# First mLSTM head: three gate projection groups issued ahead of chunk 0, each of the other nine queued on TensorE behind its own chunk

## The chip, the cores and the metric

The kernel runs on one core of one Trainium2 chip. The time is that of the device for one execution of the whole program, in microseconds; less is better. Before the change it is 1215.55 us, the median of 3 runs (1214.6 to 1216.65).

## The reference, cut to what matters

Two layers are computed on 1024 frames of a prompt and 32 frames of a running stream (1056 columns in all), width 1024. Layer 0 mixes pooling and band attention; the change doesn't touch it. Layer 1 is an mLSTM with four heads of width 256, in chunks (the kernel takes 128 frames at a time). For each head:

```
q, k, v, o, z, gates = split(rmsnorm(x) @ w_in)
b = cumsum(lf);  dmat = causal(b_t - b_s + ig_s);  m_t = max(b + m, max(dmat))
s = (q k^T) * exp(dmat - m_t)
num = a * (C q) + s v          # C: 256 x 256 state carried from chunk to chunk
h = num / max(|den|, exp(-m_t))
C = decay * C + (v * wgt)^T k
out = layernorm(h) * gain * sigmoid(o) * silu(z)
y = out @ w_out
```

The change is about the order of two kinds of TensorE work in the first head: the projections o and z (the gates of the output, needed only at the end of a head) and the chunks.

## The kernel before

Activations are kept feature-major, 128 features on the partitions and frames along the free dimension. A projection of 128 output features is done by `dense`: for each of three column groups (384, 384 and 288 frames) 24 matmuls accumulate in one PSUM bank of the pool pd (3 banks). These are 8 slices of the inner dimension, each in 3 products of high and low parts (`mm3`, L108 to L110). VectorE then takes the bank out. I call the 24 matmuls of one column group a group. Weights are loaded by `load_w`: two DMAs of 256 KB on SyncE's queue, two casts on ScalarE for the high part (L95), two subtractions for the low part on VectorE (L96); there are three buffers for them (wh, wl), so that the weights of a projection can be prepared when the projection three places ahead of it has run.

For one head of layer 1, program order is this:

- `head_qkv`: two projections each for q, k and v. After each k and each v projection `tokens` turns the result to frames on the partitions: for chunks 0 to 3, 4 to 7 and 8, it makes 4, 4 and 1 transposes on TensorE into the single bank of pool pm (L950), a copy by ScalarE (L953) and, for v, a subtraction by VectorE that forms the low part (L955). The bank is free for the next step only when the copy and the subtraction are done.
- `head_gate` puts the four gate projections o0, z0, o1, z1 on a list, as 12 steps of one group each (`later`). Nothing is issued yet. `fill` issues the next step of the list, and with a projection's first step the load of its weights.
- `head_mix`: nine chunks (the last with 32 frames). Each has the scores S (L1018: 4 matmuls), their product with the decay matrix D on VectorE, the split into a high part Sh (ScalarE, L1022) and a low part Sl (VectorE, L1023), the output pv from S and v and from the state Cp (9 matmuls, `mmv`, L985 to L987), and the state update pu (2 times 3 matmuls, `mmv`). D comes from an exponential on ScalarE (L1014) over a tile MA, which a DMA brings on SyncE's queue (3 buffers). At the end of each chunk `fill` issues one step of the list.
- `fill_all` issues what is left of the list (three steps), and `head_out` normalizes, transposes back and multiplies with the gates.

The order in which an engine issues instructions isn't program order. A planner goes through a model of the time line and lets each engine take, among the instructions that are ready in the model, the one that is earliest in program order. Steps that are later in the program but ready sooner run ahead. The order that results is fixed, and each engine keeps to it on the chip, waiting where an input is late. `tc.issue_after(ins)` takes that freedom away for one engine: what is traced inside it and runs on the engine of `ins` is placed behind `ins` in that engine's order; it doesn't wait for `ins` to end.

Other things that the prediction speaks of: q of the next head is written to the tile qT, of which there is one buffer, so q projections of head 1 can fill PSUM banks but not be taken out before head 0 has read its qT for the last time. z is written to a tile "row" (2 buffers), which v uses too ahead of its transposes.

Of the kernel before, what the change touches and what calls it, by code (L numbers as in the profile page):

```python
# [29 lines left out]
def clen(c):  # L30
    return 128 if c < 8 else DEC


class Net:
# [947 lines left out]
    def mmv(self, p, a, v, first, last):  # L982
        nc = self.nc
        (ah, al), (vh, vl) = a, v
        nc.tensor.matmul(out=p, lhsT=ah, rhs=vh, start=first, stop=False)  # L985
        nc.tensor.matmul(out=p, lhsT=ah, rhs=vl, start=False, stop=False)  # L986
        nc.tensor.matmul(out=p, lhsT=al, rhs=vh, start=False, stop=last)  # L987

    def head_mix(self, h, qT, kT, K, V):
        nc, io, lp = self.nc, self.io, self.lp  # L990
# [2 lines left out]
        st = lp.tile([128, NCH, 6], F32, name="bst", bufs=1)  # L993
        mv = lp.tile([128, NCH, 2], F32, name="bmv", bufs=1)
        C = Cp = None

        def split_C(C):
            Cp = self.split("C", [128, 2, VW], 2)
            nc.scalar.copy(out=Cp[0], in_=C)
            nc.vector.tensor_tensor(out=Cp[1], in0=C, in1=Cp[0].bitcast(F32), op=ALU.subtract)  # L1000
            return Cp
        for c in range(NCH):
            L = clen(c)
            t = slice(128 * c, 128 * c + L)
            if c == 8:
                C = lp.tile([128, 2, VW], F32, name="C", bufs=2)
                nc.sync.dma_start(out=C, in_=io["stC"][h].rearrange("(d p) v -> p d v", p=128))
                Cp = split_C(C)
            MA = lp.tile([128, 2, 128], F32, name="MA", bufs=3)
            nc.sync.dma_start(out=MA[:, :, :L], in_=self.mdr[h:h + 1, :, t].to_broadcast([128, 2, L]))  # L1010
            Mb, Ab = MA[:, 0, :L], MA[:, 1, :L]
            v = V[0][:L, c], V[1][:L, c]
            D = lp.tile([128, 128], F32, name="D", bufs=3)
            nc.scalar.activation(out=D[:L, :L], in_=Mb[:L], func=AF.Exp, scale=-1.0, bias=self.ct[:L, c, h:h + 1])  # L1014
            self.causal(D[:L, :L], L)
            ps = self.ps.tile([128, 512], F32, name="ps")
            for d in range(2):
                nc.tensor.matmul(out=ps[:L, :L], lhsT=kT[:, d, t], rhs=qT[:, d, t], start=(d == 0), stop=(d == 1))  # L1018
            S = lp.tile([128, 128], F32, name="S", bufs=2)
            Sp = [x[:L, :L] for x in self.split("S", [128, 128], 2)]  # L1020
            nc.vector.tensor_tensor(out=S[:L, :L], in0=ps[:L, :L], in1=D[:L, :L], op=ALU.mult)
            nc.scalar.copy(out=Sp[0], in_=S[:L, :L])  # L1022
            nc.vector.tensor_tensor(out=Sp[1], in0=S[:L, :L], in1=Sp[0].bitcast(F32), op=ALU.subtract)  # L1023
            pn = self.pv.tile([128, 512], F32, name="pv")[:L, 0:VW]
            self.mmv(pn, Sp, v, True, C is None)
            if C is not None:
                qa = lp.tile([128, 2, 128], F32, name="qa", bufs=2)
                qp = [x[:, :, :L] for x in self.split("qa", [128, 2, 128], 2)]
                for d in range(2):
                    nc.gpsimd.tensor_tensor(out=qa[:, d, :L], in0=qT[:, d, t], in1=Ab, op=ALU.mult)  # L1030
                nc.scalar.copy(out=qp[0], in_=qa[:, :, :L])  # L1031
                nc.gpsimd.tensor_tensor(out=qp[1], in0=qa[:, :, :L], in1=qp[0].bitcast(F32), op=ALU.subtract)  # L1032
                for d in range(2):
                    self.mmv(pn, (qp[0][:, d], qp[1][:, d]), (Cp[0][:, d], Cp[1][:, d]), False, d == 1)
            nc.scalar.copy(out=num[:L, c], in_=pn[:, 0:257])
            nc.vector.bn_stats(out=st[:, c], in_=num[:, c, 0:256])
            nc.vector.bn_aggr(out=mv[:, c], in_=st[:, c])
            wK = [x[:L] for x in self.split("wK", [128, 256], 2)]
            nc.scalar.mul(out=wK[0], in_=K[:L, c], mul=D[:L, L - 1:L])
            nc.vector.scalar_tensor_tensor(out=wK[1], in0=K[:L, c], scalar=D[:L, L - 1:L], in1=wK[0].bitcast(F32),  # L1040
                                           op0=ALU.mult, op1=ALU.subtract)
            Cn = lp.tile([128, 2, VW], F32, name="C", bufs=2)
            for d in range(2):
                ds = slice(128 * d, 128 * d + 128)
                pu = self.ps.tile([128, 512], F32, name="ps")[:, 0:VW]
                self.mmv(pu, (wK[0][:, ds], wK[1][:, ds]), v, True, True)
                if C is None:
                    nc.vector.tensor_copy(out=Cn[:, d], in_=pu)
                else:
                    nc.vector.scalar_tensor_tensor(out=Cn[:, d], in0=C[:, d], scalar=Ab[:, L - 1:L], in1=pu,  # L1050
                                                   op0=ALU.mult, op1=ALU.add)
            C = Cn
            if c < 7:
                Cp = split_C(C)
            self.fill()
            if c >= 7:
                nc.sync.dma_start(out=io["Co"][c - 7, h].rearrange("(d p) v -> p d v", p=128), in_=C[:, :, 0:257])
        return num, mv
# [232 lines left out]
```

## Time and profile before

| | |
|---|---|
| median of 3 runs | 1215.55 us (1214.6 to 1216.65) |
| the profiled execution's own time | 1215.28 us |
| its span in the profile | 1213.6 us |
| mean granted clock of TensorE | 0.991 of full speed |
| TensorE busy | 1183.3 us, 98% |
| VectorE, ScalarE, GpSimd busy | 681.2, 472.9, 298.9 us |

The span is that of the profiled execution; 1.7 us of its time lie around it. TensorE issues matmuls that overlap each other, so a matmul's duration is longer than its distance to the next, and a TensorE that is shown as busy isn't one at its peak. The granted clock is 1.00 at 2.4 GHz and 0.50 at 1.2 GHz.

### The profile page before, as it was taken

To read this page: it belongs to the slowest core of one execution; us is meant where nothing else is said; L and a number is where in the kernel's file an instruction comes from. 1 tells how busy PE (TensorE), PEld (TensorE's weight loads), DVE (VectorE), ACT (ScalarE), POOL (GpSimd) and SP (SyncE) were. 2 spreads that over 40 slices of the span, in tenths; PEclk is the share of its full clock that TensorE was granted. 3 is DMA by queue.
4 is the path that set the end of the run, shared out by engine and by line. 5 is a ranking of instruction groups with operands and counts; after the bars stand their busy time and mean duration, and the time that the engine had idled before them with its cause. 6 is when DMAs were issued, how large, how long until landed. Compare 5 with 4: busy or idle time off the path is not lost.

```text
span 1213.6 us, 19521 instructions
## 1 busy us (share of the span) xinstructions
PE 1183.3 (98%) x7457; PEld 1137.1 (94%) x7457; DVE 681.2 (56%) x1460; ACT 472.9 (39%) x980; POOL 298.9 (25%) x394
## 2 busy tenths in 40 slices
PE   7899999999999899999999999999999999999996
PEld 7899899898899799999999899999999999998996
DVE  7657476576668446774447533753247432666424
ACT  7624334443533454531334232432234322445521
POOL 1323532433241335620102300221003110123322
PEclk9999999999999999999999899999999999999998
DMA  8401121112212253321111231122111321122433
GB/s 257 125 19 54 54 82 53 54 45 67 78 36 92 80 176 105 124 94 53 54 36 53 63 101 36 52 67 98 36 51 42 76 88 36 44 77 79 128 104 130
DMA packets 79613, 94.03 MB, mean 77 GB/s; under 512 B 19208, under 2 KB 56856, under 8 KB 79520
## 3 DMA queue, kind: packets, MB, share of 16 engines
q1 hardware_dynamic: 79520, 92.79, 24.9%
q8 instruction: 58, 0.95, 0.3%
q14 instruction: 35, 0.29, 0.1%
HBM read 72.64 MB, written 21.69 MB: 78 GB/s over the span
## 4 chain that ended last, share of the span: by engine, by line
PE 95%; ACT 1%; DMA 1%; DVE 1%; issue 1%; POOL 1%; SPq 0%; DVEq 0%; POOLq 0%; ACTq 0%
PE pd L108 25%; PE pd L110 25%; PE pd L109 25%; PE pv L406 4%; PE ps L354 1%; PE pm L950 1%; PE ps L355 1%; PE ps L1018 1%; PE pv L985 1%; PE pv L987 1%; PE pv L986 1%; PE ps L985 1%; PE ps L986 1%; PE ps L987 1%; PE pm L176 1%
## 5 line engine op out<-in xcount | busy, mean ns | idle before, releaser
L108 PE MATMUL pd<-xh,wh 128*128 128x384 f32 (+1 forms) x1864 | 610.2, 328 | 9.4 <-ACT wh L95 7.8
L110 PE MATMUL pd<-xh,wl 128*128 128x384 f32 (+1 forms) x1864 | 607.5, 326 | 0.1
L109 PE MATMUL pd<-xl,wh 128*128 128x384 f32 (+1 forms) x1864 | 607.1, 326 | 0.1
L108 PEld LDWEIGHTS pd<-xh,wh 128*128 128x128 f32 x1864 | 352.4, 189 | 13.6 <-ACT wh L95 8.1
L109 PEld LDWEIGHTS pd<-xl,wh 128*128 128x128 f32 x1864 | 352.6, 189 | 2.6 <-POOL xl L203 0.3
L110 PEld LDWEIGHTS pd<-xh,wl 128*128 128x128 f32 x1864 | 352.3, 189 | 2.4 <-DVE wl L96 0.7
L95 ACT CAST wh<-wr 128x512 fp32r<-128x512 f32 x158 | 91.4, 619 | 154.6 <-PE pd L109 109.6
L96 DVE TENSOR_TENSOR wl<-wr,wh 128x512 fp32r<-128x512 f32 x116 | 78.2, 701 | 22.1 <-ACT wh L95 20.5
L96 POOL TENSOR_TENSOR wl<-wr,wh 128x512 fp32r<-128x512 f32 x42 | 55.7, 1342 | 83.4 <-DMA extr<-ext 27.4
L194 POOL TENSOR_TENSOR acc<-acc,sqt 128x384 f32<-128x384 f32 (+1 forms) x41 | 43.5, 1062 | 88.2 <-ACT sqt L193 88.1
L1032 POOL TENSOR_TENSOR qal<-qa,qah 128x256 fp32r<-128x256 f32 (+1 forms) x32 | 27.5, 863 | 141.1 <-ACT qah L1031 130.3
L75 POOL TENSOR_SCALAR_AFFINE_SELECT D<-D 128x128 f32<-128x128 f32 (+1 forms) x36 | 12.2, 340 | 181.2 <-ACT D L1014 168.1
L406 PE MATMUL pv<-st,vt 128*128 128x512 f32 (+1 forms) x192 | 55.1, 433 | 0.9 <-ACT rg L415 0.9
L406 PEld LDWEIGHTS pv<-st,vt 128*128 128x128 f32 x192 | 35.0, 189 | 20.3 <-issue 10.6
L263 DVE TENSOR_TENSOR row<-pd,r 128x384 f32<-128x384 f32 (+1 forms) x36 | 18.3, 520 | 59.4 <-PE pd L110 59.3
L372 ACT ACTIVATE st<-ps,far 128x256 f32<-128x256 f32 (+3 forms) x56 | 27.1, 489 | 50.0 <-DVE st L364 34.0
L1050 DVE SCALAR_TENSOR_TENSOR C<-C,MA,ps 128x258 f32<-128x258 f32 x64 | 30.4, 478 | 28.8 <-PE ps L987 17.8
L265 DVE SCALAR_TENSOR_TENSOR kT<-pd,r 128x384 f32<-128x384 f32 (+1 forms) x24 | 12.6, 524 | 57.4 <-PE pd L110 57.3
L395 DVE TENSOR_TENSOR st<-st,mb 128x512 f32<-128x512 f32 (+1 forms) x96 | 39.3, 485 | 8.3 <-POOL mb L699 8.3
L1030 POOL TENSOR_TENSOR qa<-qT,MA 128x128 f32<-128x128 f32 (+1 forms) x64 | 26.9, 439 | 66.1 <-DVE qT L263 35.9
L364 DVE TENSOR_TENSOR st<-ps,B 128x256 f32<-128x256 f32 (+1 forms) x72 | 25.3, 371 | 24.7 <-PE ps L355 24.3
L1085 ACT ACTIVATE hn<-num,n_u,n_y 128x256 f32<-128x256 f32 (+1 forms) x36 | 20.4, 596 | 40.9 <-PE pv L1087 34.3
(305 smaller groups left out, 1681.5 us busy)
## 6 DMA issues: line engine op xcount, KB each, us to landing
wr<-in_w SPq DMA_DIRECT2D x128, 256.0 KB, 3.0
xr<-mix SPq DMA_DIRECT2D x26, 192.0 KB, 2.5
wr<-in_w0o SPq DMA_DIRECT2D x16, 256.0 KB, 3.2
MA<-mdr SPq DMA_DIRECT2D x32, 128.0 KB, 3.5
wr<-in_w1o SPq DMA_DIRECT2D x16, 256.0 KB, 3.3
x<-in_x SPq DMA_DIRECT2D x16, 192.0 KB, 2.8
x<-x1d SPq DMA_DIRECT2D x16, 192.0 KB, 3.5
out_y<-y SPq DMA_DIRECT2D x16, 192.0 KB, 2.0
```

The lines of the kernel that those rows point to most:

```text
L95: nc.scalar.copy(out=wh[:, k], in_=wr)
L96: eng.tensor_tensor(out=wl[:, k], in0=wr, in1=wh[:, k].bitcast(F32), op=ALU.subtract)
L108: nc.tensor.matmul(out=p, lhsT=wh[:, k], rhs=xh[:, k], start=first and i == 0, stop=False)
L109: nc.tensor.matmul(out=p, lhsT=wh[:, k], rhs=xl[:, k], start=False, stop=False)
L110: nc.tensor.matmul(out=p, lhsT=wl[:, k], rhs=xh[:, k], start=False, stop=last and i == len(ks) - 1)
L194: (eng or nc.gpsimd).tensor_tensor(out=acc, in0=acc, in1=t[:, :n], op=ALU.add)
L372: nc.scalar.activation(out=st[:, off + a:off + b], in_=p[:, a:b], func=AF.Identity, bias=far)
L395: nc.vector.tensor_tensor(out=dst, in0=dst, in1=mb[:, a - q0:b - q0], op=ALU.subtract)
L406: nc.tensor.matmul(out=pv[:, a - q0:b - q0], lhsT=vt[:, j, 64 * e:64 * e + 128], rhs=dst, start=(i == 0), stop=(i == len(order) - 1))
L1030: nc.gpsimd.tensor_tensor(out=qa[:, d, :L], in0=qT[:, d, t], in1=Ab, op=ALU.mult)
L1032: nc.gpsimd.tensor_tensor(out=qp[1], in0=qa[:, :, :L], in1=qp[0].bitcast(F32), op=ALU.subtract)
L1050: nc.vector.scalar_tensor_tensor(out=Cn[:, d], in0=C[:, d], scalar=Ab[:, L - 1:L], in1=pu, op0=ALU.mult, op1=ALU.add)
```

## The change

Ahead of chunk 0 of the first head three steps of the list are issued in program order (the whole of o0). After that, each chunk of this head issues one step as before, but its matmuls are placed on TensorE behind the last matmul of the chunk's state update (`self.pe`, the last of the three of `mmv`). With nine chunks the twelve steps of the list are all gone at the end of chunk 8. Heads 1 to 3 stay as they were.

```diff
@@ mmv
-        nc.tensor.matmul(out=p, lhsT=al, rhs=vh, start=False, stop=last)
+        self.pe = nc.tensor.matmul(out=p, lhsT=al, rhs=vh, start=False, stop=last).ins
@@ head_mix
         C = Cp = None
+        if h == 0:
+            self.fill(3)
...
             if c < 7:
                 Cp = split_C(C)
-            self.fill()
+
+            with self.tc.issue_after(self.pe) if h == 0 else nullcontext():
+                self.fill()
             if c >= 7:
```

## Rows read from the trace of the kernel before

**Rows 1.** The page: span; chain that ended last, by engine.

```profile
span 1213.6 us, 19521 instructions
PE 95%; ACT 1%; DMA 1%; DVE 1%; issue 1%; POOL 1%; SPq 0%; DVEq 0%; POOLq 0%; ACTq 0%
```

**Rows 2.** Stretches of head 0: us, TensorE busy (matmuls), clock, DMA share, GB/s.

```profile
610.45:633.84 23.39, 22.74 (x145) 1.00 0.13 46
655.90:674.50 18.60, 18.60 (x139) 1.00 0.16 45
674.50:682.75 8.25, 5.23 (x31) 0.82 0.62 166
```

**Rows 3.** Waits of TensorE from 580 to 720 us: total, times, longest.

```profile
PE pv L985 <- ACT Sh L1022: 2.4, 2, 1.8
PE pd L108 <- DVE row L276: 0.7, 1, 0.7
PE ps L985 <- DVE S L1021: 0.6, 1, 0.6
```

**Rows 4.** Stretches of 2 us at the end of head 0's chunks, TensorE.

```profile
676.00:678.00 2.00, 0.29 (x3) 1.00 0.80 248
678.00:680.00 2.00, 1.89 (x14) 0.93 0.47 99
680.00:682.00 2.00, 1.49 (x6) 0.50 0.98 249
682.00:684.00 2.00, 1.88 (x6) 0.50 0.25 81
684.00:686.00 2.00, 2.00 (x8) 0.50 0.35 116
686.00:688.00 2.00, 2.00 (x11) 0.87 0.76 59
```

**Rows 5.** Time line of ScalarE around chunk 7: start, us, idle before and releaser.

```profile
677.47 0.40 ACT L1014 ACTIVATE D<-MA,g_c 128x128 f32<-128x128 f32 x1 [2.23 <-DMA MA<-mdr]
677.77 0.28 ACT L1022 CAST Sh<-S 128x128 fp32r<-128x128 f32 x1
```

**Rows 6.** Time line of VectorE: q of head 1 taken out of PSUM.

```profile
679.08 1.34 DVE L263 TENSOR_TENSOR qT<-pd,r 128x384 f32<-128x384 f32 x3
```

**Rows 7.** Time line of TensorE: o0's last matmul, transposes, chunk 0's first product.

```profile
610.31 0.29 PE L110 MATMUL pd<-xh,wl 128*128 128x288 f32 x1
...
611.49 0.27 PE L950 MATMUL pm<-ident,kT 128*32 128x128 f32 x1
...
615.45 0.60 PE L950 MATMUL pm<-ident,row 128*128 128x128 f32 x4
...
629.57 0.60 PE L950 MATMUL pm<-ident,row 128*128 128x128 f32 x4
...
633.84 0.28 PE L985 MATMUL pv<-Vh,Sh 128*128 128x258 f32 x1
```

**Rows 8.** Time line of ScalarE: copies of V after transposes.

```profile
616.08 0.59 ACT L953 CAST Vh<-pm 128x512 fp32r<-128x512 f32 x1 [3.94 <-PE pm L950]
...
639.81 0.26 ACT L953 CAST Vh<-pm 32x128 fp32r<-32x128 f32 x1 [0.77 <-PE pm L950]
```

**Rows 9.** Time line of VectorE: low parts of V.

```profile
616.70 0.69 DVE L955 TENSOR_TENSOR Vl<-pm,Vh 128x512 fp32r<-128x512 f32 x1 [4.24 <-ACT Vh L953]
640.10 0.28 DVE L955 TENSOR_TENSOR Vl<-pm,Vh 32x128 fp32r<-32x128 f32 x1
```

**Rows 10.** Stretches of 2 us in layer 0, TensorE: another thin patch.

```profile
52.00:54.00 2.00, 1.01 (x8) 1.00 1.09 268
54.00:56.00 2.00, 1.10 (x4) 0.77 0.74 204
56.00:58.00 2.00, 2.00 (x8) 0.50 0.40 148
58.00:60.00 2.00, 2.00 (x12) 0.88 0.00 0
```

## The prediction, made before the change was run

> **What bounds the kernel now.** I read the page first: the chain that ended last is TensorE for 95% of the span [rows 1]. So a change of order gains only where TensorE stands idle or runs at half clock, and loses where it makes such places. I then took stretches of TensorE's busy time through layer 1, and in head 0 found one patch: from 674.50 to 682.75 us it is busy for 5.23 of 8.25 us, at a mean clock of 0.82, while the 18.60 us ahead of it are full [rows 2]. The waits of TensorE name the pieces [rows 3]: 0.6 us for S, 2.4 us in two waits for Sh, and far ahead, at 623 us, 0.65 us (0.7 in the row; it is also 23.39 less 22.74 in [rows 2]) for a PSUM bank.
>
> ScalarE's time line explains the Sh wait: the exponential of D for a chunk of head 1 is placed in front of Sh and sits 2.23 us until the DMA of its MA has landed [rows 5]. Such waits exist earlier too, but TensorE then had other groups to issue. Here it has none: the twelve steps of the list ran long ago, under K's and V's transposes and the first chunks, and the three groups of head 1's q that stood in for them fill all three PSUM banks until they are taken out at 679.08 [rows 6].
>
> Behind the idle time the clock falls to 0.50, through 686 and a little beyond [rows 4]. From the rows: 0.07 x 2 x 2 = 0.28 us at half in the second row, 6.0 in the next three, 0.13 x 2 x 2 = 0.52 in the last, 6.8 in all, in which TensorE is busy for 0.28 + 5.37 + 0.52 = 6.2 us; half of that, 3.1 us, is lost to the clock.
>
> So what the change can win in head 0 is 3.0 us of idle time (8.25 less 5.23), 3.1 us of clock and 0.65 us at 623: **6.75 us**.
>
> **The change part by part.** No instruction is added or removed. Nine groups of 24 matmuls (z0, o1, z1) move on TensorE behind the chunks; o0 keeps its place, since it ran right behind v already, with its last matmul at 610.31 [rows 7].
>
> *The end of the chunks.* Each chunk now has a group behind it, chunks 6, 7 and 8 too, and head 1's q can be used on top. The exponential that waits for MA still holds Sh up, but 24 matmuls at the mean distance of the full stretch, 18.60 / 139 = 0.13 us [rows 2], are 3.2 us and cover 2.23. The wait at 623 was z0 needing the "row" buffer of v; z0 now starts when v has long been transposed. Bounds for what comes back: 0 to 6.75 us. I take **6.0**: near the upper end, because the nearest full rows, 655.90 to 674.50, have the same chunks with q's groups between them and no idle time [rows 2], and less than all of it because the last chunk also fetches its state by DMA.
>
> *The front.* From 610.45 to 633.84 us TensorE is full today, with 145 matmuls and 0.65 us of idle time [rows 2], because z0 and much of o1 run there between the transposes. Chunk 0's first product with V is at 633.84 [rows 7]. It needs the transposes of K's end and of V, which go through one bank step by step. At 610.45 five steps are still to come: K of chunk 8 (611.49), the first half's V of chunks 0 to 3 (615.45), of 4 to 7 and of 8, then the second half's V of chunks 0 to 3 (629.57) [rows 7]. Today there is a group or so between two steps, which costs nothing as it is work that must be done. After the change those groups must not go ahead of chunk 0's state update, and no other projection is ready: head 1's q needs the weight buffers of z0. So TensorE waits for the steps themselves. Their price, from rows:
>
> - K of chunk 8: transpose 0.27, a copy as long as V's of the same size, 0.26 [rows 7, 8], with hand-over about 0.6.
> - V of four chunks: transposes start at 615.45, the copy at 616.08, the subtraction ends at 616.70 + 0.69 = 617.39 [rows 7 to 9]: 1.94. Twice: 3.9.
> - V of chunk 8: 0.27, then from 639.81 to 640.10 + 0.28 [rows 8, 9]: about 0.9.
> - V of the second half, to the end of the copy: 616.08 + 0.59 - 615.45 = 1.2.
>
> That is 6.6 us; with 0.3 for weight casts that ScalarE has to do when o0 ends (the third buffer is then free), 6.9 us, so chunk 0's product starts at about 617.4. TensorE works in it for 2 x 0.27 + 3 x 0.60 = 2.3 us, and idles for 4.6. Then products with V's low part wait for the subtraction, which ends 0.72 after the copy and is covered by three products of 0.13 each: 0.3 more. **Idle: 4.9 us.** Lower bound: 4.0, if steps move up a little among o0's matmuls; upper bound 7, if casts and the tanh of o0 get in front of each copy.
>
> *The clock behind it.* TensorE will be busy for a third of 7 us. From 52 to 56 us it was busy for 1.01 and 1.10 of 2 us each, and the clock fell: 0.23 x 4 + 2.0 + 0.12 x 4 = 3.4 us at half [rows 10], which costs 1.7 us once the work is dense. The end of the chunks cost 3.1 [rows 4]. Bounds: 0 to 3.1. I take **1.9**, near the first, as here too dense work (chunk 0 and a group of z0) follows at once. The Trainium skill, "TensorE: Matmul & The Clock Gate", section "Why this matters for your kernels", warns of long idle gaps between bursts of matmuls; by that rule the clock would hold here, where no single gap should be longer than about 1.4 us, and the sum would be without the 1.9 us. The rows differ: the longest single wait ahead of the fall at 680 was 1.8 us [rows 3, 4], little more than that.
>
> *What moves with the groups.* Each projection brings two weight DMAs, two casts and two subtractions; z0, o1 and z1 now end 10 to 20 us later, so the loads for head 1 that wait for their buffers go later too, on the same SyncE queue as the MA loads; and VectorE and ScalarE get the gate work (one multiplication and a tanh, for z two more on VectorE) in every chunk rather than in the first four. In the time up to 655.9 they carried it beside chunks without a wait of TensorE [rows 3]. Bounds: 0 to 2 us, I take 0.4. GpSimd has nothing of it.
>
> **Sum:** + 4.9 + 1.9 + 0.4 - 6.0 = **+ 1.2 us**. On the profiled execution's 1215.28 us that is 1216.5; that execution was 0.3 us below the median of the runs shown, so I forecast 1216.8 us.
>
> **The rivals.**
>
> *A, the forecast:* the patch at the end is mended and another one, of the same size, is made in front of chunk 0. By the bounds of the front (4.0 to 7, clock 1 to 3.1, the fall itself being sure in this case) and of the end (5 to 6.75): 1215.55 + 4.0 + 1 - 6.75 = 1213.8 to 1215.55 + 7 + 3.1 - 5 = 1220.7. Chance 0.46.
>
> *B, no gap in front; faster.* The five steps are placed among o0's matmuls, so that V is ready at 611. Then the 6.75 us come back nearly whole: 1215.55 - 6 = 1209.5. It decides if at least four of the five steps stand ahead of 610.3 on TensorE. Against it: the steps come one in 4 to 5 us wherever groups are there to be issued [rows 7], and only some 12 us of o0 lie there. Chance 0.13.
>
> *C, the chunks are thinner than I think; slower.* Between S and pv of a chunk the groups must bridge ScalarE's wait for MA. If a group stands on the wrong side, each chunk pays up to 1.8 us as chunk 7 did [rows 3]. Three or four such waits, with the clock falling again, take all or most of the end's 6.75 us back; the front's 4.9 + 1.9 stay lost. With 1 us either way that is + 5.8 to + 7.8: 1221 to 1223.5. For it: the DMA's landing is later than the planner holds (a wait of 2.23 us [rows 5]). Against it: the full 18.60 us [rows 2]. Point of decision: idle time of TensorE over 3 us between chunk 1 and chunk 8. Chance 0.28.
>
> *D, as A, but the clock holds in the front.* Short transposes keep it up: 1216.8 - 1.9 = 1214.9. For it: busy bursts every 2 us; against it [rows 4, 10]. Chance 0.13.
>
> **How the numbers follow.** About 0.2%, 2.4 us, is what a measurement of this kernel can tell from no change: 1213.1 to 1218.0 is the same. Of A's 0.46 I put 0.30 inside and 0.16 above. B is faster (0.13). C is slower, but for 0.02. D is the same, but for 0.01 faster. Faster 0.14, same 0.44, slower 0.42. The range leaves out B and the upper part of C: 1213 to 1222. A by itself is 1213.8 to 1220.7.
>
> **What would show it.** In the changed profile TensorE should be thin, at about a third, for 7 us right behind o0's last matmul, with transposes 2 us apart and waits named after the low part of V or its copy; chunk 0's first product should be near 617 rather than 633.8; the clock should show 0.50 for 3 to 4 us behind that. From chunk 1 on groups should alternate with chunks, and the waits for Sh at the end should be gone, with head 1's first projections at full clock. The prediction is wrong if the front is full (B), if waits of over 3 us in all stand between chunks 1 and 8 (C), or if the clock stays at 1.00 (D).

## The result, and the profile after

The changed kernel takes **1226.02 us** (median of 5 runs, 1225.75 to 1227.56), the kernel before on the same chip 1216.56 us (1214.6 to 1217.38): ratio 1.0082 [1.0068, 1.0096], about 9.5 us slower. The forecast was 1216.8 us with a range of 1213 to 1222. The profiled execution took 1226.02 us, its span is 1224.3 us, 10.7 us longer than before [rows 1].

The page of the kernel after: span, and the chain that ended last, by engine.

```profile
span 1224.3 us, 19523 instructions
PE 92%; DMA 2%; ACT 2%; DVE 2%; issue 1%; POOL 1%; SPq 0%; DVEq 0%; POOLq 0%; ACTq 0%
```

TensorE's share of the chain fell from 95% to 92%. Its waits from 560 to 760 us in the kernel after (the two new lines in `head_mix` push the numbers below them up by 2, so that S is now L1023):

```profile
PE ps L985 <- DVE S L1023: 5.7, 5, 3.2
PE pm L950 <- DVE Vl L955: 3.5, 3, 1.4
PE pm L950 <- ACT K L953: 1.1, 1, 1.1
PE pv L985 <- ACT Vh L953: 0.7, 1, 0.7
```

The three lower lines are the forecast front: 5.3 us of waits for the steps of K and V. The wait for Sh [rows 3] is gone. The first line is new in its size: the state update waits five times for S, 5.7 us in all, where it waited once for 0.6 us.

TensorE's time line of the kernel after, at those waits (start, duration, instruction, idle time before it and its releaser):

```profile
608.61 0.29 PE L110 MATMUL pd<-xh,wl 128*128 128x288 f32 x1
608.74 0.27 PE L950 MATMUL pm<-ident,kT 128*32 128x128 f32 x1
610.15 0.66 PE L950 MATMUL pm<-ident,row 128*128 128x128 f32 x4 [1.14 <-ACT K L953]
612.21 1.11 PE L950 MATMUL pm<-ident,row 128*128 128x128 f32 x4 [1.40 <-DVE Vl L955]
614.73 0.40 PE L950 MATMUL pm<-ident,row 128*32 128x128 f32 x1 [1.40 <-DVE Vl L955]
615.78 1.12 PE L950 MATMUL pm<-ident,row 128*128 128x128 f32 x4 [0.66 <-DVE Vl L955]
617.57 0.58 PE L985 MATMUL pv<-Vh,Sh 128*128 128x258 f32 x1 [0.67 <-ACT Vh L953]
...
652.18 0.61 PE L1020 MATMUL ps<-qT,kT 128*128 128x128 f32 x4
652.54 0.37 PE L985 MATMUL ps<-Vh,wKh 128*128 128x258 f32 x1
...
652.87 0.28 PE L987 MATMUL ps<-Vh,wKl 128*128 128x258 f32 x1
654.28 0.38 PE L985 MATMUL ps<-Vh,wKh 128*128 128x258 f32 x1 [1.14 <-DVE S L1023]
...
676.58 0.54 PE L985 MATMUL ps<-Vh,wKh 32*128 32x258 f32 x1 [3.18 <-DVE S L1023]
```

Chunk 0's first product starts at 617.57 instead of 633.84 [rows 7]. At 652.18 one sees the new wait in full, in chunk 5. The scores of the chunk fill one of the two PSUM banks of the pool ps, the first product of its own state update the other. The second product of the update needs a bank again, and the one it gets is that of the scores, free only when VectorE has read them for S. Nothing else stands in TensorE's order between the two products: the group of this chunk is held behind the second one.

TensorE in stretches of 2 us in the kernel after (busy time with its matmuls, granted clock, DMA share, GB/s):

```profile
610.00:612.00 2.00, 0.66 (x4) 0.95 0.39 122
612.00:614.00 2.00, 1.11 (x4) 0.50 0.41 140
614.00:616.00 2.00, 0.61 (x2) 0.50 0.00 0
616.00:618.00 2.00, 1.33 (x6) 0.50 0.00 0
618.00:620.00 2.00, 2.00 (x11) 0.50 0.00 0
620.00:622.00 2.00, 2.00 (x9) 0.50 0.04 8
622.00:624.00 2.00, 2.00 (x13) 0.99 0.00 0
...
676.00:678.00 2.00, 1.42 (x5) 0.66 0.00 0
678.00:680.00 2.00, 2.00 (x10) 0.50 0.46 139
680.00:682.00 2.00, 2.00 (x10) 0.50 0.81 31
682.00:684.00 2.00, 2.00 (x9) 0.63 0.25 27
```

*Front:* 0.05 x 2 x 2 + 10.0 + 0.01 x 2 x 2 = 10.2 us at half clock, in which TensorE is busy for 0.2 + 1.11 + 0.61 + 1.33 + 4.0 = 7.2 us at most; half of about 7.1 is 3.5 us lost. *End:* a wait of 3.18 us, and then 0.34 x 2 x 2 + 4.0 + 0.37 x 2 x 2 = 6.8 us at half, all busy: 3.4 us lost. Before, the same place had 3.0 us of idle time and 3.1 us of clock [rows 2, 4].

So the sum as measured is: front + 5.3 idle + 3.5 clock; update's waits in four chunks 5.74 - 3.18 = + 2.6; end + 3.18 + 3.4 against the 6.75 us that were there to win, - 0.2. That is **+ 11.2 us**, beside 10.7 us of span and 9.5 us between the medians.

That these agree so well is partly luck. The profiled execution of the changed kernel was 1.7 us ahead before the change could act: the first column group of v is taken out of PSUM (VectorE, L263) at 582.45, before at 584.16, and o0's last matmul ran at 608.61 instead of 610.31 [rows 7]. From that take-out of v to the same one of head 1, at 739.22 and before at 728.35, it is 156.77 us in place of 144.19, so the stage itself became 12.6 us longer. The 1.4 us that the sum lacks stand in no idle time. An estimate of where they are: the last matmul ahead of the wait at 654.28 counts as busy for 0.28 us, where such matmuls follow each other in about 0.12 when TensorE is dense, and the changed kernel has ten waits in place of four.

What made the last S late is in the order of three engines. SyncE's time line in the kernel after, at chunk 8:

```profile
670.94 0.47 SPq L1009 DMA_DIRECT2D C<-in_stC  x1
```

ScalarE's time line of the same kernel, at the high part of the state:

```profile
674.29 0.62 ACT L1001 CAST Ch<-C 128x516 fp32r<-128x516 f32 x1 [2.42 <-DMA C<-in_stC]
```

VectorE's time line of the same kernel, from the low part of the state to S of chunk 8:

```profile
674.95 0.69 DVE L1002 TENSOR_TENSOR Cl<-C,Ch 128x516 fp32r<-128x516 f32 x1 [2.40 <-ACT Ch L1001]
...
676.36 0.16 DVE L1023 TENSOR_TENSOR S<-ps,D 32x32 f32<-32x32 f32 x1
```

The load of the stream's state is issued at 670.94. ScalarE stands 2.42 us until it has landed, VectorE 2.40 us for ScalarE's high part, and S of chunk 8, 0.16 us long, is queued behind that on VectorE, with a step of the gate work and the statistics of the chunk before it in between. TensorE's second product waits for S, and the last group for that product.

### The profile page after: what moved, and what is told of

Its sections match the earlier page's. It is cut to its first block, busy times and chain, and to the rows that moved or that the text cites. A ratio compares the mean times of both kernels' runs of the same rounds, so it can differ in the third digit from the quotient of the medians.

```text
span 1224.3 us, 19523 instructions
## 1 busy us (share of the span) xinstructions
PE 1187.2 (97%) x7457; PEld 1139.2 (93%) x7457; DVE 675.8 (55%) x1460; ACT 473.2 (39%) x980; POOL 297.7 (24%) x394
## 4 chain that ended last, share of the span: by engine, by line
PE 92%; DMA 2%; ACT 2%; DVE 2%; issue 1%; POOL 1%; SPq 0%; DVEq 0%; POOLq 0%; ACTq 0%
PE pd L108 24%; PE pd L110 24%; PE pd L109 24%; PE pv L406 4%; PE pm L950 1%; PE ps L354 1%; DMA MA<-mdr 1%; PE ps L355 1%; PE ps L1020 1%; PE pv L985 1%; PE pv L987 1%; PE pv L986 1%; PE ps L985 1%; PE ps L986 1%; PE ps L987 1%
## 5 line engine op out<-in xcount | busy, mean ns | idle before, releaser
L108 PEld LDWEIGHTS pd<-xh,wh 128*128 128x128 f32 x1864 | 353.4, 190 | 12.6 <-ACT wh L95 8.3
L95 ACT CAST wh<-wr 128x512 fp32r<-128x512 f32 x158 | 91.5, 619 | 156.4 <-PE pd L109 114.7
L406 PEld LDWEIGHTS pv<-st,vt 128*128 128x128 f32 x192 | 35.0, 190 | 20.0 <-issue 10.8
L263 DVE TENSOR_TENSOR row<-pd,r 128x384 f32<-128x384 f32 (+1 forms) x36 | 18.3, 520 | 60.6 <-PE pd L110 60.4
L265 DVE SCALAR_TENSOR_TENSOR kT<-pd,r 128x384 f32<-128x384 f32 (+1 forms) x24 | 12.6, 524 | 63.1 <-PE pd L110 63.1
L1016 ACT ACTIVATE D<-MA,g_c 128x128 f32<-128x128 f32 (+1 forms) x36 | 14.1, 393 | 61.9 <-DMA MA<-mdr 61.7
```

The lines of the kernel that those rows point to most:

```text
L95: nc.scalar.copy(out=wh[:, k], in_=wr)
L108: nc.tensor.matmul(out=p, lhsT=wh[:, k], rhs=xh[:, k], start=first and i == 0, stop=False)
L406: nc.tensor.matmul(out=pv[:, a - q0:b - q0], lhsT=vt[:, j, 64 * e:64 * e + 128], rhs=dst, start=(i == 0), stop=(i == len(order) - 1))
```

## The experiments

Each was timed beside the kernel before on the same chip. Diffs are against the changed kernel unless said otherwise.

**1. The order without the hold.** Three groups are traced ahead of chunk 0, but no group is tied to its chunk.

```diff
-            with self.tc.issue_after(self.pe) if h == 0 else nullcontext():
+            with nullcontext():
```

> Three steps are issued ahead of chunk 0, but no group is held behind its chunk. Theory 1 (the holding back costs everything: 8.8 us in front of chunk 0, 2.5 us between the chunks, and the patch at chunk 8 is neither mended nor made worse): the groups run ahead as in the kernel before, 1216 to 1217 us. Theory 2 (the earlier place of the three steps in program order has a cost of its own): clearly above 1217.

Measured: 1215.03 us beside 1215.65 us, ratio 0.9998 [0.9988, 1.0008]. The new program order alone costs nothing and wins nothing: in its trace the wait for Sh is there again, 2.2 us, and the clock falls behind it (0.76 and 0.73 in the two stretches of 10 us from 670 to 690). All of the loss comes with the hold.

**2. Six groups ahead, with the hold.**

```diff
-            self.fill(3)
+            self.fill(6)
```

> Six steps ahead of chunk 0 (o0 and z0), the other six held behind chunks 0 to 5, nothing behind 6 to 8. Theory 1: z0 covers the transposes of V, so the front's 8.8 us come back; the end has only head 1's q left and keeps its patch: 1217 to 1220 us. If the front is bound by something other than the missing groups, TensorE stays thin ahead of chunk 0 and the time above 1222.

Measured: 1218.6 us beside 1215.65, ratio 1.0024 [1.0014, 1.0034]: over half of the loss is gone. The time lies within the expected 1217 to 1220, but neither half of the theory holds. The front isn't full; and the end, which was to keep its patch, is: TensorE is busy from 670 to 690 us without a gap at a clock of 1.00, with q of head 1, which nothing holds, taken out of PSUM at 683.77, 686.58 and 688.12. The waits of TensorE from 560 to 760 us in this kernel begin with:

```profile
PE pm L950 <- DVE Vl L955: 3.4, 2, 3.0
```

The three groups of z0 now run between the transposes of V, and then there is nothing again until the last step: one wait of 3.0 us in place of several. The steps come as late as before, as they are placed between groups; to issue more groups ahead moves the gap behind them and makes it shorter. The update's wait for S is still there, 1.8 us in three chunks.

**3. The state's own buffer.** In chunk 8 the state is loaded into a tile of its own, so that the load doesn't wait for the buffer of the carried state.

```diff
-                C = lp.tile([128, 2, VW], F32, name="C", bufs=2)
+                C = lp.tile([128, 2, VW], F32, name="C8", bufs=1)
```

> The changed kernel, with the stream's state for chunk 8 loaded into a buffer of its own, so that its DMA need not wait for chunk 7. Theory 1 (S of chunk 8 stands on VectorE behind the split of that state, which waits for the DMA, and the last group stands behind both): the wait of 3.2 us and the 3.2 us of half clock behind it go, 1219 to 1221 us. Rival (the last group is late because it is held behind chunk 8, whatever the state does): the wait stays, 1225 to 1227.

Measured: 1224.31 us beside 1215.65, ratio 1.0067 [1.0052, 1.0082], between the ranges of the theory and of its rival. Against the changed kernel's 1.0082, taken on another chip, the intervals overlap, so that this says little by itself; I ran it again beside the unaltered changed kernel.

> The changed kernel once more, beside the next three on one chip, as their measure: 1225 to 1227 us by both theories.

> The changed kernel with the state of chunk 8 in a buffer of its own, beside the changed kernel on the same chip. Theory 1: the first profile of it had no wait and no half clock at chunk 8, so 4 to 6.5 us less than the changed kernel. Rival (something later takes most of it back): less than 3 us.

Measured on one chip, with the kernel before at 1216.01: changed kernel 1227.95, ratio 1.0102 [1.0089, 1.0115], a little above the 1225 to 1227 expected; with the state's own buffer 1222.91, ratio 1.0064 [1.0051, 1.0077]. So it wins 5.0 us. The wait of the update for S in the unaltered kernel of this pair:

```profile
PE ps L985 <- DVE S L1023: 5.8, 5, 2.8
```

The same line with the state's own buffer:

```profile
PE ps L985 <- DVE S L1023: 2.5, 4, 1.0
```

With the buffer the long wait is gone, TensorE is busy and at full clock from 670 to 690 us, and the four short waits between the chunks stay. The late state was what set off the end's loss (experiments 5 and 6 show that it needs the hold as well); that the held last group makes a gap there by itself, with or without the state, is refuted. The span is still 1220.4 us, 6.8 us more than before: TensorE's idle time from 540 to 870 us is 8.1 us against 3.7, and the clock costs about 3.8 (in the front alone) against 3.1, together 5.1. The other 1.7 us stand in no idle time, as the 1.4 us above.

**4. Six ahead, later groups only from chunk 3 on, the state's own buffer.**

```diff
-            self.fill(3)
+            self.fill(6)
...
-                C = lp.tile([128, 2, VW], F32, name="C", bufs=2)
+                C = lp.tile([128, 2, VW], F32, name="C8", bufs=1)
...
-                self.fill()
+                self.fill(1 if h or c >= 3 else 0)
```

> Six steps ahead of chunk 0, the other six held behind chunks 3 to 8, and the state of chunk 8 in a buffer of its own. Theory 1: front and end are both covered, 1226.0 - 8.8 - 6.4 = 1210.8, say 1210 to 1213 us, faster than before. Rival (the end's patch is not the state's DMA): 1216 to 1219.

Measured: 1220.55 us beside 1215.65, ratio 1.0038 [1.0025, 1.0051]. A miss of both ranges: the front keeps its wait of 3.0 us, and the first chunks, now without groups, are thin too. From 630 to 640 us TensorE is busy for 8.40 us at a mean clock of 0.80. The end is full. Work that is saved for the end is missing ahead of it.

**5. The hold on chunk 0 alone.** All nine groups are placed behind chunk 0's update and are otherwise free.

```diff
-            with self.tc.issue_after(self.pe) if h == 0 else nullcontext():
+            if c == 0:
+                first = self.pe
+            with self.tc.issue_after(first) if h == 0 else nullcontext():
```

> The nine groups are all held behind chunk 0's state update, and free after it. Theory 1: the front stays as in the changed kernel (5.3 us idle, 3.5 us of clock), the 2.5 us between chunks go, and the end is mended or as before: 1218 to 1224 us. Rival (the holding behind each single chunk is the main cost): within 2 us of the kernel before.

Measured: 1217.12 us beside 1216.01, ratio 1.0009 [1.0000, 1.0017]. All waits of TensorE from 560 to 760 us in this kernel:

```profile
PE pm L950 <- DVE Vl L955: 3.5, 3, 1.4
PE pm L950 <- ACT K L953: 1.1, 1, 1.1
PE pv L985 <- ACT Vh L953: 0.7, 1, 0.7
```

Its stretches of 10 us around the front, and at the end of the chunks:

```profile
610.00:620.00 10.00, 4.90 (x21) 3.56 (x21) 3.85 (x7) 3.27 (x8) 0.00 (x0) 0.62 0.15 52
620.00:630.00 10.00, 10.00 (x57) 9.93 (x56) 5.52 (x14) 2.97 (x7) 0.00 (x0) 0.87 0.01 2
670.00:680.00 10.00, 10.00 (x64) 8.74 (x64) 6.21 (x17) 4.06 (x10) 0.59 (x2) 1.00 0.70 127
680.00:690.00 10.00, 10.00 (x66) 9.97 (x65) 4.84 (x18) 2.24 (x4) 2.68 (x3) 1.00 0.10 36
```

(Columns: length, busy time of TensorE, its weight loads, VectorE, ScalarE and GpSimd, granted clock, DMA share, GB/s.) The front has the same waits as in the changed kernel, and 0.38 x 20 + 0.13 x 20 = 10.2 us at half clock as there. Between the chunks and at the end nothing is left, and the end's 6.75 us came back whole: 5.3 + 3.5 - 6.75 = + 2.1 us, against + 1.1 [0, 2.1] measured. The first theory, 1218 to 1224 us, missed, and its rival held: the holding behind each single chunk is the main cost. This kernel did what the forecast said of the changed one.

**6. The hold in each chunk, on another instruction.** A group is placed behind its chunk's scores, not behind its state update.

```diff
-                nc.tensor.matmul(out=ps[:L, :L], lhsT=kT[:, d, t], rhs=qT[:, d, t], start=(d == 0), stop=(d == 1))
+                score = nc.tensor.matmul(out=ps[:L, :L], lhsT=kT[:, d, t], rhs=qT[:, d, t], start=(d == 0), stop=(d == 1)).ins
...
-            with self.tc.issue_after(self.pe) if h == 0 else nullcontext():
+            with self.tc.issue_after(score) if h == 0 else nullcontext():
```

> As the changed kernel, but each group is held behind its chunk's scores instead of behind the last matmul of its state update. Theory (the place of the hold is the cost: a group held behind the update can't stand between the scores and the update, where TensorE waits for the product S): the waits for S between chunks and at chunk 8 go, only the front's stay, 1216 to 1219 us. Rival (one group for each chunk is too little, wherever it is held): 1222 to 1228.

Measured: 1216.12 us beside 1216.05, ratio 1.0007 [0.9998, 1.0016]. All waits of TensorE from 560 to 760 us in this kernel:

```profile
PE pm L950 <- DVE Vl L955: 3.9, 4, 1.4
PE pv L985 <- ACT Vh L953: 0.7, 1, 0.7
```

Its time line of TensorE in one chunk:

```profile
638.95 0.29 PE L987 MATMUL ps<-Vh,wKl 128*128 128x258 f32 x1
639.08 0.34 PE L108 MATMUL pd<-xh,wh 128*128 128x384 f32 x1
...
640.65 0.34 PE L108 MATMUL pd<-xh,wh 128*128 128x384 f32 x1
640.82 0.29 PE L985 MATMUL ps<-Vh,wKh 128*128 128x258 f32 x1
```

Between the first product of the update and the second now stand 10 matmuls of a group, 640.82 - 639.08 = 1.7 us, and the second doesn't wait. The groups are still tied one by one to the chunks, and chunk 8 still loads its state into the old buffer; neither a wait between chunks nor the one of 3.18 us is there. What cost the time between the chunks and at the end was the instruction behind which the group was held, the last one of the chunk. That the wait is for the bank is read from its releaser and the two banks of the pool; a third bank for ps was not tried.

The front is cheaper here too, so the end and the chunks alone don't make the whole difference of some 9 us. Chunk 0's scores run early, so its group may run ahead of chunk 0's product, and it does: its 24 matmuls stand between 609.68 and 613.99, right behind o0. The front has 4.6 us of idle time and 3.4 us at half clock, in place of 5.3 and 10.2.

**7. More groups ahead, with the hold on chunk 0 alone.** Experiment 5 with six groups ahead of chunk 0, as in the diff, and in a second kernel with nine, `self.fill(9)`.

```diff
-            self.fill(3)
+            self.fill(6)
...
+            if c == 0:
+                first = self.pe
+            with self.tc.issue_after(first) if h == 0 else nullcontext():
```

> Six steps ahead of chunk 0, the other six held behind chunk 0's update alone, free after it. Theory (groups spent in the front are missing at the end): front about 4 us idle with 2.4 us of clock, as in the run with six ahead; the end nearly covered: 1214 to 1218 us. Rival (the end needs all nine): 1219 to 1222.

> Nine steps ahead of chunk 0, the last three held behind chunk 0's update alone. Theory: front full as in the kernel before, end open as in the kernel before: 1215 to 1217.5 us.

Measured, both beside 1216.05: six 1215.85, ratio 1.0007 [0.9998, 1.0016]; nine 1214.0, ratio 0.9985 [0.9975, 0.9994], 1 us below its range. With six the wait of 3.0 us of experiment 2 is there and the end is full. With nine the front is full, and the end is thin again. Its stretches at the end (columns as above):

```profile
670.00:680.00 10.00, 7.18 (x52) 6.03 (x51) 8.57 (x24) 4.44 (x15) 2.12 (x6) 1.00 0.27 71
680.00:690.00 10.00, 10.00 (x60) 9.22 (x59) 3.92 (x15) 2.65 (x7) 3.62 (x8) 1.00 0.57 114
```

2.8 us are idle, about as in the kernel before (3.0), but this execution, at 1211.5 us the fastest of its 11, shows no fall of the clock. Whether a gap goes to the front or to the end, it is about as large; no split among three, six and nine closes both.

**8. One more buffer for MA.** First in the kernel before, then in the kernel with nine ahead.

```diff
-            MA = lp.tile([128, 2, 128], F32, name="MA", bufs=3)
+            MA = lp.tile([128, 2, 128], F32, name="MA", bufs=4)
```

> The kernel before with four MA buffers in place of three, so that the MA of head 1's first chunks can be fetched a chunk earlier. Theory 1 (the patch at the end of head 0 is ScalarE waiting for MA in front of Sh): it goes in part or whole, 1210 to 1214 us. Rival (there is simply no work left for TensorE): another wait takes its place, 1215 to 1217.

> Nine steps ahead of chunk 0, three held behind chunk 0's update, and four MA buffers. Theory (what is left at the end is ScalarE waiting for MA in front of Sh, 1.9 us, and a clock that may or may not fall behind it): 1210 to 1213.5 us, the fastest so far. Rival (another wait takes the place): 1213.5 to 1215.

Measured: kernel before with 4 buffers 1214.5 beside 1216.01, ratio 0.9985 [0.9974, 0.9995]; nine ahead with 4 buffers **1213.12** beside 1215.58, ratio 0.9979 [0.9970, 0.9988], the lowest median of all, and faster than the kernel before and the changed one. Its interval overlaps that of nine ahead with 3 buffers, taken on another chip, so the times don't show what the buffer adds there. The wait for Sh is gone in both. Others stand in part in its place, beside those for row and S that were there before [rows 3]; the waits of the kernel before with 4 buffers begin with a new one:

```profile
PE ps L985 <- DVE C L1050: 0.9, 1, 0.9
```

TensorE is idle for 1.8 us there from 670 to 680, against 3.0 in the patch before [rows 2]: the late MA was one of several causes, each of which shows where no group is left to cover it.

## Why the prediction was wrong

**The step that failed** is the end of the chunks: of a possible 6.75 us the prediction let 6.0 come back. 0.2 us came back. The reasoning was that a group of 3.2 us behind each chunk would cover a wait of 2.23 us. Behind, it doesn't: the wait that now ends last lies inside the chunk, between the two products of the update (L985), and a group held behind the second of them can't stand there (held behind the scores, in experiment 6, the same groups leave no wait there). The full stretch that I took for the nearest row [rows 2] had groups that were free to go to that place. TensorE's time line of the kernel before, from the scores of a chunk to the second product of its update:

```profile
658.11 0.61 PE L1018 MATMUL ps<-qT,kT 128*128 128x128 f32 x4
...
660.73 0.28 PE L987 MATMUL ps<-Vh,wKl 128*128 128x258 f32 x1
660.85 0.34 PE L108 MATMUL pd<-xh,wh 128*128 128x384 f32 x1
...
662.42 0.28 PE L985 MATMUL ps<-Vh,wKh 128*128 128x258 f32 x1
```

What the prediction left out is the PSUM bank of the scores; the wait for it was in [rows 3] with 0.6 us, put down as a piece of the end.

In chunk 8 this wait was 3.18 us long, because the state's load stood in front of S on ScalarE and VectorE, and the clock fell behind it. The prediction had named the state, "the last chunk also fetches its state by DMA", and gave it less than a microsecond of the 6.75; with the hold it was worth 5.0 us (experiment 3).

**The other chunks.** The same wait costs 2.6 us in four of them (0.37, 0.74, 1.14 and 0.31 us), for which the prediction had no term of its own. What it took for the work that moves with the groups was 0.4 us, with bounds of 0 to 2. The gate work has a part in these waits: VectorE takes a gate group out of PSUM ahead of each of the four S. Its time line in the kernel after, in the chunk with 1.14 us:

```profile
653.51 0.53 DVE L1115 TENSOR_TENSOR go<-pd,r 128x384 f32<-128x384 f32 x1
653.95 0.28 DVE L1023 TENSOR_TENSOR S<-ps,D 128x128 f32<-128x128 f32 x1
```

But in experiments 5 and 6 the gate work moves as well and TensorE doesn't wait there, so the place of the hold makes it a cost; no run sizes the gate work alone.

**The front** held as a mechanism. 4.9 us of idle time were forecast (4.0 to 7) and 5.3 measured. That chunk 0's product, forecast for about 617.4, started at 617.57 is luck: from o0's end to it were to be 6.9 us and were 8.7, and the execution was 1.7 us ahead. The idle time is one part of that; transposes at half clock, 1.1 us for 0.6, are another. For weight casts 0.3 us were allowed, and ScalarE had 1.14 us of them (L95, at 608.81) in front of the copy of K. The clock behind it was mis-sized: 1.9 us taken, 3.1 the upper bound, 3.5 measured. I had priced it by a patch with 3.4 us at half [rows 10]. Here half clock lasted 10.2 us, through most of the thin stretch and for 4.4 us of dense work behind 617.57. The Trainium skill, "TensorE: Matmul & The Clock Gate", section "Why this matters for your kernels", warns of long idle gaps between bursts; by that rule a front with no wait over 1.40 us would have held the clock. The trace doesn't agree: 0.95 and then 0.50 while transposes came every 1 to 2.5 us.

**The rivals.** B and D fell: the front isn't full, and its clock fell. C's point of decision was passed, 5.7 us of idle time against 3 between the chunks, and its picture, a group on the wrong side of a chunk's wait, is near to what happened. But it named pv's wait for Sh and the late MA, and it gave 1221 to 1223.5; the waits for Sh are gone in the profile after, the place was the update, and with the front's clock above its bound the time went past C's end. A came true in another kernel, that of experiment 5, with the same front and all of the end back.

**Head 1's q** was to be used on top at the end. It wasn't: its first projection is taken out of PSUM at 689.34, behind the patch, while before it was at 679.08 [rows 6]. Its weights were ready early, with their cast at 639.19. In experiment 2, with no group held behind chunks 6 to 8, it was used so. Why the planner didn't place it in the gap of the changed kernel was not tried and stays open.

## What to carry to other kernels

A filler covers a wait only if it can stand at the place of the wait: tie it to the earliest instruction of the step that it must not overtake (the scores here) and not to the last, and look which wait lies between the two. Before a tie is put into every step of a loop, try it on the first step alone; the difference (1227.95 against 1217.12 here, 10.8 us on one chip) is what the later ties cost. And a fixed amount of filler work that is saved for one thin place is missing in another: count the need of all of them, then shorten the waits themselves (a fourth buffer for MA, the state's own buffer).

## What was not expected of the hardware

- The clock doesn't follow idle time alone. In the changed kernel 5.3 us of idle time in the front, in five waits, came with 10.2 us at 0.50. In experiment 6 the front had 4.6 us of idle time and 3.4 us at half. In experiment 7, with nine ahead, 2.8 us of waits at the end came with no fall, and in the kernel before 3.0 us of them with 6.8 us at half [rows 2, 4]. I have no rule from these rows that fits all four.
- The fourth buffer for MA made the times spread: 12 runs from 1210.99 to 1217.3 us, where those of experiment 6 lie within 1215.72 to 1217.62. The profiled one, at 1214.69 us, had a fall of the clock (0.82 and 0.67 in the two stretches from 670 to 690); the mean granted clock was 0.991 in it, 0.994 in the two fastest and 0.987 and 0.988 in the two slowest. That the fastest had no fall there is an inference.
